# Trailing-window sums of the pooling branch on VectorE instead of GpSimd, issued 28 passes behind their product

## The chip, the cores and the metric

The kernel runs on one NeuronCore of a Trainium2 chip. The core has a matrix engine (TensorE, PE in the profile), a vector engine (VectorE, DVE), an activation engine (ScalarE, ACT), a general-purpose engine (GpSimd, POOL) and a queue engine that issues the loads (SyncE, SP). Each of them works through its own instructions strictly in order, and they wait for one another through semaphores. The metric is the device time of one execution in microseconds (us), as the median of several runs.

## The reference

Two layers of a streaming encoder over 512 tokens of 1024 channels in float32. Each layer is a feed-forward block, a mixer and another feed-forward block. The mixer adds up three branches, each behind a gate; the change lies in branch B, the pooling one:

```
def multiscale_pool(u, w_pool, pool_scale):        # u = h @ w_in[:, columns of B], 512 columns
    for g, w in enumerate((2, 4, 8, 16)):          # four groups of 128 channels
        # mean of the last w tokens (fewer at the start), minus the token itself
        diffs.append((upper - lower) / count - uf[:, :, sl])
    y = jnp.einsum('bsgc,gce->bsge', d, w_pool)    # one 128 x 128 map for each group
    return y * pool_scale
...
branch = jnp.einsum('bsnw,nwd->bsnd', ys, w_branch)
gates = jax.nn.sigmoid(g_lin.reshape(B, S, N_BRANCHES, D_MODEL))
merged = jnp.sum(gates * branch, axis=2)
return merged @ w_out
```

## The kernel before

Channels lie on the 128 partitions and tokens on the free axis, so a tile is 128 x 512. To keep float32 accuracy on TensorE, every operand is split in two parts, a rounded one (`whi`, `hhi`) and the rest (`wlo`, `hlo`), and each product takes three matmuls (`triple`, L119 to L121). A 128-column product over 1024 channels is eight triples, or 24 matmuls; the code counts a matmul of 512 columns as one pass in `pe[0]`.

`wchunk` brings one block of weights: a load into `raw` (two buffers), a ScalarE cast to `whi` (L277) and a VectorE subtraction to `wlo` (L279). `whi` and `wlo` have three buffers each. The sums of the products stand in PSUM tiles called `acc`, of which there are four.

`later(n, fn)` puts a piece of work on a list, and `poll`, called before every triple, runs whatever is due once `n` passes have been recorded. Behind this recording stands a scheduler that sets the final order of each engine's instructions by priorities; so the order on an engine is not the order of the code.

At the end of each mixer stand, in this order: the four pooling groups (`pool_front`), the merge of branch C (`merge_units(l, 2, ...)`: for each of eight column blocks a gate product of 24 passes and a branch product of 12) and the merge of branch B. A pooling group is a product into an `acc` tile; a ScalarE copy of it to `u` (L1027), with 16 zero columns ahead; log2(w) additions of `u` with itself shifted by 1, 2, 4, 8 columns (L1033, tiles `strip`, two buffers), that is 1, 2, 3 and 4 additions for the groups 0 to 3; the division and the difference (L1037 to L1040); a split into `ptb` (L384, L385). Sixty passes later `pool_back` multiplies it by its map (three matmuls into another `acc` tile), and ScalarE and VectorE empty that tile (L1050, L1051).

In the same stretch the kernel works ahead on the modulation of later blocks: `mod_step` loads 512 KB of `w_ada` into a tile `b` and reduces it on VectorE (L206). These loads stand in the same SP queue as the weight loads.

The chosen lines of the change:

```
        nc.scalar.copy(u[:, 16:], pu)
...
            nc.gpsimd.tensor_tensor(nx[:, 16:], cur[:, 16:], cur[:, 16 - step:T + 16 - step], op=ALU.add)
...
            for gi in range(4):
                b = pool_front(l, gi)
                later(60, lambda gi=gi, b=b: pool_back(l, gi, b, wp, yb))
```

Of the kernel before, what the change touches and what calls it, by code (L numbers as in the profile page):

```python
# [19 lines left out]
ALU = mybir.AluOpType  # L20
# [3 lines left out]
T = 512  # L24
# [11 lines left out]
WINDOWS = (2, 4, 8, 16)  # L36
# [4 lines left out]
def encoder_kernel(tc, xT, c, w_ada, b_ada, gains, w_gate, w_up, w_down, w_qkv, w_f, w_ubg,  # L41
                   qk_gain, rel, fbias, w_pool, pool_scale, w_branch, w_out, inv_cnt, w_first, out):
    nc = tc.nc
# [54 lines left out]
    def later(delay, fn, group=None):  # L98
        t = Task(pe[0] + delay, fn, group)
        tasks.append(t)  # L100
        return t
# [160 lines left out]
    def wchunk(src, shape, side=True, spare=None, lo_eng=None):  # L262
        lo_eng = lo_eng or nc.vector
        side_work(side)
        raw = st([P] + list(shape), F32, *(("b", NB) if spare else ("raw", NRAW)))
        last["dma"] = nc.sync.dma_start(raw, src).ins
        if spare == "ptb":
            both = st([P, 2] + list(shape), F32R, "ptb", 2)
            hi, lo = both[:, 0], both[:, 1]
        elif spare == "b":  # L270
            hi = st([P] + list(shape), F32R, "b", NB)
            lo = st([P] + list(shape), F32R, "b", NB)
        else:
            hi = st([P] + list(shape), F32R, "whi", 3)
            lo = st([P] + list(shape), F32R, "wlo", 3)
        with behind("scalar"):
            nc.scalar.copy(hi, raw)  # L277
        with behind("vector"):
            lo_eng.tensor_tensor(lo, raw, hi.bitcast(F32), op=ALU.subtract)  # L279
        return hi, lo  # L280
# [735 lines left out]
    LAG_T, LAG_V = 30, 14  # L1016


    def pool_front(l, g):
        w = WINDOWS[g]  # L1020
        hi, lo = wchunk(w_ubg[l, g], (KD, P))
        pu = acc()
        for k in range(KD):
            triple(pu, hi[:, k, :], lo[:, k, :], hhi[:, k, :], hlo[:, k, :], k == 0, k == KD - 1)
        u = st([P, T + 16], F32, "b", NB)
        nc.gpsimd.memset(u[:, :16], 0.0)
        nc.scalar.copy(u[:, 16:], pu)  # L1027
        cur = u
        step = 1
        while step < w:  # L1030
            nx = st([P, T + 16], F32, "strip", 2)
            nc.gpsimd.memset(nx[:, :16], 0.0)
            nc.gpsimd.tensor_tensor(nx[:, 16:], cur[:, 16:], cur[:, 16 - step:T + 16 - step], op=ALU.add)  # L1033
            cur = nx
            step *= 2
        hd = st([P, 16], F32, "hd", 1)
        nc.vector.tensor_tensor(hd, cur[:, 16:32], icnt[:, g, :], op=ALU.mult)  # L1037
        df = st([P, T], F32, "ssum", 1)
        nc.vector.scalar_tensor_tensor(df[:, 16:], cur[:, 32:], 1.0 / w, u[:, 32:], op0=ALU.mult, op1=ALU.subtract)
        nc.vector.tensor_tensor(df[:, :16], hd, u[:, 16:32], op=ALU.subtract)  # L1040
        b = st([P, 2, T], F32R, "ptb", 2)
        split_to(b[:, 0, :], b[:, 1, :], df)
        return b

    def pool_back(l, g, b, wp, ys):
        py = acc()
        triple(py, wp[0][:, g, :], wp[1][:, g, :], b[:, 0, :], b[:, 1, :], True, True)
        y = blk("b")
        sc = psc[:, l, g:g + 1]
        nc.scalar.activation(y[:, 0, :], py, AF.Identity, scale=sc)  # L1050
        nc.vector.scalar_tensor_tensor(y[:, 1, :], py, sc, y[:, 0, :].bitcast(F32), op0=ALU.mult, op1=ALU.subtract)  # L1051
        ys.append(y)
# [9 lines left out]
    def merge_units(l, n, ys, put):  # L1062
        wb = [None]
        gates = {}

        def gate_of(d):
            if d % 2 == 0:
                wb[0] = wchunk(w_branch[l, n, d:d + 2].rearrange("a p k c -> p a k c"), (2, 4, P))
            gh, gl = wchunk(w_ubg[l, 4 + n * KD + d], (KD, P))
            pg = gates[d] = acc()  # L1070
            for k in range(KD):
                triple(pg, gh[:, k, :], gl[:, k, :], hhi[:, k, :], hlo[:, k, :], k == 0, k == KD - 1)
                yield

        for d in range(KD):
            if d not in gates:
                yield from gate_of(d)
            if n == 0 and d == 0:
                yield from gate_of(1)
            pg = gates[d]  # L1080
            bh, bl = wb[0]
            th = t1(T)
            nc.scalar.activation(th, pg, AF.Tanh, scale=0.5)
            pb = acc()
            if n == 0 and d == 0:
                poll(group="a")
            for k in range(4):
                triple(pb, bh[:, d % 2, k, :], bl[:, d % 2, k, :], ys[k][:, 0, :], ys[k][:, 1, :], k == 0, k == 3)
                yield
            put(d, pb, th)  # L1090
# [6 lines left out]
    class Mixer:  # L1097
# [10 lines left out]
        def run(self, nxt):  # L1108
            l = self.l
            in_ffn[0] = False  # L1110
            for b in range(4):
                nc.gpsimd.dma_start(x_dram[b], x_blocks[b].rearrange("p a t -> p (a t)"))
            g = qkgc[:, l, :]
            g8 = qg8[:, l, :]
            qa, ka, va, qc, kc, vc = [], [], [], [], [], []
            ya, yb, yc = [], [], []
            drain(proj_qk(l, 0, g8[:, 0:1], True, qa, self.pre, self.norm),
                  proj_qk(l, 1, g[:, 1:2], False, ka), forget(l),
                  proj_v(l, 2, "xv", va))
            finish_turns()  # L1120
            turns.clear()
            heads[0] = 0

            def fill_a():
                yield from proj_qk(l, 3, g8[:, 2:3], True, qc)
                yield from proj_qk(l, 4, g[:, 3:4], False, kc)
                yield from proj_v(l, 5, "v2", vc)

            attention(qa, ka, va, lambda h: strip_a(l, h), ya, fill_a(), FILL_A, "a")
            heads[0] = H  # L1130

            m = []

            def put_a(d, pb, th):
                if d % 2 == 0:
                    m.append(blk("xv", F32))
                nc.vector.scalar_tensor_tensor(m[d // 2][:, d % 2, :], th, 1.0, pb, op0=ALU.add, op1=ALU.mult)

            def put_c(d, pb, th):
                md = m[d // 2][:, d % 2, :]  # L1140
                tmp = t2(T)
                nc.vector.scalar_tensor_tensor(tmp, th, 1.0, pb, op0=ALU.add, op1=ALU.mult)
                nc.gpsimd.tensor_tensor(md, md, tmp, op=ALU.add)

            mh = []

            def put_b(d, pb, th):
                put_c(d, pb, th)
                b = blk("v2" if d < 4 else "b")
                split_to(b[:, 0, :], b[:, 1, :], m[d // 2][:, d % 2, :])  # L1150
                mh.append(b)

            ubs = {}

            def fill_c():
                yield from merge_units(l, 0, ya, put_a)

            attention(qc, kc, vc, lambda h: strip_c(l, h), yc, fill_c(), FILL_C, "c")
            finish_turns()
            turns.clear()  # L1160
            poll(True)
            silc[0] = st([P, D], F32, "b", NB)
            nc.sync.dma_start(silc[0], sil_dram.broadcast_to([P, D]))
            wp = wpool_load(l)
            mc = merge_units(l, 2, yc, put_c)
            for gi in range(4):
                b = pool_front(l, gi)
                later(60, lambda gi=gi, b=b: pool_back(l, gi, b, wp, yb))
            in_ffn[0], mod_tag[0], MOD_RATE[0] = True, "b", 1.0
            drain(mc)  # L1170
            poll(True)
            mb = merge_units(l, 1, yb, put_b)
            drain(mb)
            in_ffn[0], mod_tag[0] = False, "raw"

            for b in range(4):
                xb = blk("xv", F32)
                nc.sync.dma_start(xb, x_dram[b].rearrange("p (a t) -> p a t", a=2))
                x_blocks[b] = xb
            mod_need(l, 5)  # L1180
            for c0 in (0, T):
                def src(c):
                    return w_out[l, 2 * c * P:(2 * c + 2) * P, c0:c0 + T].rearrange("(k p) c -> p k c", p=P)

                def ops(hi, lo, kt, j):
                    return (hi[:, j * P:(j + 1) * P], lo[:, j * P:(j + 1) * P], mh[kt][:, 0, :], mh[kt][:, 1, :])

                if c0 == 0:
                    nxt.prefetch("b")
                for j, hs, o in k_outer(src, 4, ops, nxt.prefetch_weights if c0 else None):  # L1190
                    d = c0 // P + j
                    residual_tail(d, hs, o, modc[:, l, 5, d:d + 1], nxt)
# [69 lines left out]
```

## Time and profile before

| what | value |
|---|---|
| time, median of 3 runs | 2403.73 us (2403.13 to 2406.02) |
| time of the profiled execution | 2404.73 us |
| its span | 2403.0 us |
| granted TensorE clock | 1.00 |
| busy: PE, DVE, ACT, POOL | 2359.9, 1725.9, 1198.4, 351.7 us |
| the pooling additions (L1033), both layers | 20 on POOL, 1.04 to 1.90 us each |
| loads over the span | 320.94 MB, mean 134 GB/s |

Busy time is the union of the instructions' spans on an engine. A row of the timeline gives start, length, engine, line, operation, tiles (written <- read) and shape; in square brackets at its end stands how long the engine sat idle before it and who ended that. Matmuls overlap in the pipeline: one of 512 columns is shown as 0.39 us long, but in a stretch without waits the next one starts 0.23 us after it. A time lost on PE is therefore read from the distance of two starts.

### The profile page before, as it was taken

Reading aid. Unit: us, or ns where it says so; the run is one execution under the profiler, and the core shown is the slowest. Engines: PE = TensorE matmul, PEld = TensorE weight load, DVE = VectorE, ACT = ScalarE, POOL = GpSimd, SP = SyncE. Lnnn points to the kernel's source line nnn. Section 1 sums busy time; section 2 is a strip of 40 time slices with the busy share of each in tenths; the row PEclk is TensorE's granted clock in tenths of the full one; section 3 lists DMA queues with packets and bytes.
Section 4 is the critical chain, followed back from the end, with each engine's and each line's share of the span. In section 5 each row is a group of like instructions: output and inputs, shape, how many; then the busy total and the mean of one; then the engine's idle time right before and its main releaser. Section 6 shows DMA issues by size and latency. Waiting matters only on the chain. (4 is left out here: it accounts for less than half of the span.)

```text
span 2403.0 us, 36815 instructions
## 1 busy us (share of the span) xinstructions
PE 2359.9 (98%) x14106; PEld 2085.6 (87%) x14106; DVE 1725.9 (72%) x3070; ACT 1198.4 (50%) x2090; POOL 351.7 (15%) x423
## 2 busy tenths in 40 slices
PE   7999999999999999999999999999999999999999
PEld 5799998778878898989998989978787788989898
DVE  8988866787665476878677878577866655658583
ACT  5353555786632353535553626466865324536252
POOL 3000011144432210000100000102444322000000
PEclk9999999999999999999999999999999999999999
DMA  7736342323345424353325353423233554223322
GB/s 274 238 113 228 99 152 84 93 79 109 108 171 201 175 98 166 105 186 105 132 83 196 104 197 106 141 79 98 80 116 108 193 182 169 71 97 106 101 96 103
DMA packets 116438, 320.94 MB, mean 134 GB/s; under 512 B 11139, under 2 KB 13315, under 8 KB 116261
## 3 DMA queue, kind: packets, MB, share of 16 engines
q1 hardware_dynamic: 115106, 314.38, 38.7%
q0 software_dynamic: 1152, 4.19, 0.4%
q8 instruction: 111, 1.82, 0.3%
q14 instruction: 67, 0.54, 0.1%
q10 hardware_dynamic: 2, 0.00, 0.0%
HBM read 312.16 MB, written 6.38 MB: 133 GB/s over the span
## 5 line engine op out<-in xcount | busy, mean ns | idle before, releaser
L277 ACT CAST whi<-raw 128x1024 fp32r<-128x1024 f32 (+1 forms) x267 | 277.4, 1043 | 431.5 <-PE acc L120 217.9
L279 DVE TENSOR_TENSOR wlo<-raw,whi 128x1024 fp32r<-128x1024 f32 x259 | 319.4, 1237 | 162.2 <-ACT whi L277 159.0
L119 PE MATMUL acc<-b,whi 128*128 128x512 f32 (+1 forms) x960 | 360.7, 376 | 0.2 <-DVE xv L434 0.2
L121 PE MATMUL acc<-b,wlo 128*128 128x512 f32 (+1 forms) x960 | 356.7, 372 | 1.8 <-DVE wlo L279 1.8
L120 PE MATMUL acc<-b,whi 128*128 128x512 f32 (+1 forms) x960 | 357.1, 372 | 0.0
L121 PEld LDWEIGHTS acc<-b,wlo 128*128 128x128 f32 x960 | 180.8, 188 | 34.0 <-DVE wlo L279 2.6
L119 PEld LDWEIGHTS acc<-b,whi 128*128 128x128 f32 x960 | 180.8, 188 | 31.8 <-DVE xv L434 0.6
L120 PEld LDWEIGHTS acc<-b,whi 128*128 128x128 f32 x960 | 181.0, 189 | 29.8
L119 PE MATMUL acc<-hhi,whi 128*128 128x512 f32 x480 | 191.3, 400 | 6.8 <-DVE b L1051 3.1
L121 PE MATMUL acc<-hhi,wlo 128*128 128x512 f32 x480 | 188.1, 393 | 1.0 <-DVE wlo L279 1.0
L120 PE MATMUL acc<-hlo,whi 128*128 128x512 f32 x480 | 188.6, 393 | 0.2 <-DVE hlo L711 0.2
L384 ACT CAST ptb<-v 128x1024 fp32r<-128x1024 f32 x128 | 134.0, 1050 | 97.7 <-DVE v L452 56.2
L385 DVE TENSOR_TENSOR ptb<-v,ptb 128x1024 fp32r<-128x1024 f32 x128 | 156.3, 1223 | 33.8 <-ACT ptb L384 32.3
L384 ACT CAST whi<-raw 128x1024 fp32r<-128x1024 f32 (+1 forms) x128 | 106.7, 834 | 92.1 <-PE acc L120 41.9
L119 PE MATMUL acc<-whi,hhi 128*128 128x512 f32 x336 | 137.8, 411 | 0.9 <-DVE xv L385 0.9
L206 DVE CUSTOM_DVE_ANT_0 v<-v,b,badac 128x1024 f32<-128x1024 f32 x96 | 127.1, 1333 | 15.0 <-DMA v<-in_w_ada_dram 14.8
L121 PE MATMUL acc<-whi,hlo 128*128 128x512 f32 x336 | 131.9, 393 | 0.0
L120 PE MATMUL acc<-wlo,hhi 128*128 128x512 f32 x336 | 131.6, 392 | 0.0
L385 DVE TENSOR_TENSOR wlo<-raw,whi 128x1024 fp32r<-128x1024 f32 (+1 forms) x128 | 121.6, 950 | 6.5 <-ACT whi L384 5.0
L434 DVE SCALAR_TENSOR_TENSOR xv<-acc,modc,xv 128x512 f32<-128x512 f32 (+1 forms) x112 | 77.3, 690 | 62.2 <-PE acc L121 62.0
L119 PEld LDWEIGHTS acc<-hhi,whi 128*128 128x128 f32 x480 | 90.6, 189 | 25.6 <-DVE b L1051 4.0
L329 POOL TENSOR_TENSOR ssum<-ssum,t 128x256 f32<-128x256 f32 (+1 forms) x45 | 46.5, 1034 | 442.8 <-ACT t L328 442.7
(315 smaller groups left out, 6667.5 us busy)
## 6 DMA issues: line engine op xcount, KB each, us to landing
v<-in_w_ada_dram SPq DMA_DIRECT2D x96, 512.0 KB, 5.3
raw<-in_w_down_dram SPq DMA_DIRECT2D x88, 512.0 KB, 3.7
raw<-in_w_up_dram SPq DMA_DIRECT2D x82, 512.0 KB, 4.0
raw<-in_w_gate_dram SPq DMA_DIRECT2D x79, 512.0 KB, 3.7
raw<-in_w_ubg_dram SPq DMA_DIRECT2D x56, 512.0 KB, 3.6
b<-in_w_ada_dram SPq DMA_DIRECT2D x48, 512.0 KB, 4.6
raw<-in_w_qkv_dram SPq DMA_DIRECT2D x42, 512.0 KB, 3.9
raw<-in_w_branch_dram SPq DMA_DIRECT2D x24, 512.0 KB, 3.7
```

The source lines that it names most:

```text
L119: mm(o, lh, rh, start=start, stop=False)
L120: mm(o, lh, rl, start=False, stop=False)
L121: mm(o, ll, rh, start=False, stop=stop)
L206: dot = nc.vector.tensor_tensor_reduce(out=raw, in0=raw, in1=silc[0], scale=1.0, scalar=badac[:, l, j, d:d + 1], op0=ALU.mult, op1=ALU.add ...
L277: nc.scalar.copy(hi, raw)
L279: lo_eng.tensor_tensor(lo, raw, hi.bitcast(F32), op=ALU.subtract)
L329: nc.gpsimd.tensor_tensor(self.ssum[:, cols], self.ssum[:, cols], q, op=ALU.add)
L384: nc.scalar.copy(hi, src)
L385: nc.vector.tensor_tensor(lo, src, hi.bitcast(F32), op=ALU.subtract)
L434: nc.vector.scalar_tensor_tensor(x, acc_j, gate, x, op0=ALU.mult, op1=ALU.add)
```

## The change

`pool_front` is cut in two. `pool_in` holds the product, the zero columns and the ScalarE copy to `u`; it is recorded for the four groups directly one after the other. The rest (`pool_front` with `u`, run by `pooled`) is recorded 28 passes after the end of the group's product, and `pool_back` 30 passes after that instead of 60 after the product. The additions go to VectorE; the small memsets of the zero columns stay on GpSimd.

```diff
-    def pool_front(l, g):
-        w = WINDOWS[g]
+    def pool_in(l, g):
         hi, lo = wchunk(w_ubg[l, g], (KD, P))
         pu = acc()
...
         nc.scalar.copy(u[:, 16:], pu)
+        return u
+
+    def pool_front(l, g, u):
+        w = WINDOWS[g]
         cur = u
...
-            nc.gpsimd.tensor_tensor(nx[:, 16:], cur[:, 16:], cur[:, 16 - step:T + 16 - step], op=ALU.add)
+            nc.vector.tensor_tensor(nx[:, 16:], cur[:, 16:], cur[:, 16 - step:T + 16 - step], op=ALU.add)
...
+            us = []
+
+            def pooled(gi):
+                b = pool_front(l, gi, us[gi])
+                later(30, lambda: pool_back(l, gi, b, wp, yb))
+
             for gi in range(4):
-                b = pool_front(l, gi)
-                later(60, lambda gi=gi, b=b: pool_back(l, gi, b, wp, yb))
+                us.append(pool_in(l, gi))
+                later(28, lambda gi=gi: pooled(gi))
```

From the copy to `u` on, line numbers of the changed kernel differ: the copy is L1026, the addition L1036, the difference L1040 to L1043, the emptying of `pool_back`'s tile L1053 (ScalarE) and L1054 (VectorE), the emptying of a gated branch product L1145.

What the scheduler makes of it is seen engine by engine. On PE all matmuls stand in the same sequence as before: four products of 24 with `pool_back` of group 0 in the middle of the fourth, then the first gate product with that of group 1 in it, the first branch product with that of group 2, the second gate product with that of group 3. VectorE's queue is what moves.

VectorE before, layer 0, from the split of group 2 to the emptying of group 1's tile. `wlo_1510` is the weight of the second gate product, `strip_1487` the last sum of group 3, `acc_1500` the tile of group 1's map, and `b_1491` and `b_1495` are `w_ada` loads:

```order
L385 TENSOR_TENSOR ptb_1476_7250<-ssum_1475_7247,ptb_1476_7250 128x512
L279 TENSOR_TENSOR wlo_1510_7395<-raw_1508_7392,whi_1509_7394 128x1024
L206 ISA b_1491_7314,modc_123<-b_1491_7314,b_1444_7102,badac_104 128x1024
L206 ISA modc_123 128x1
L206 ISA b_1495_7323,modc_123<-b_1495_7323,b_1444_7102,badac_104 128x1024
L206 ISA modc_123 128x1
L1037 TENSOR_TENSOR hd_1488_7306<-strip_1487_7303,icnt_111 128x16
L1039 SCALAR_TENSOR_TENSOR ssum_1489_7308<-strip_1487_7303,b_1483_7291 128x496
L1040 TENSOR_TENSOR ssum_1489_7308<-hd_1488_7306,b_1483_7291 128x16
L1051 SCALAR_TENSOR_TENSOR b_1501_7346<-acc_1500_7342,psc_109,b_1501_7346 128x512
L385 TENSOR_TENSOR ptb_1490_7311<-ssum_1489_7308,ptb_1490_7311 128x512
L279 TENSOR_TENSOR wlo_1520_7454<-raw_1518_7451,whi_1519_7453 128x1024
```

VectorE now, the same place. The sums of group 3 are `strip_1497` to `strip_1500`, the tile of group 1's map is `acc_1493`, and the `w_ada` loads are `b_1478` and `b_1482`:

```order
L385 TENSOR_TENSOR ptb_1492_7313<-ssum_1491_7310,ptb_1492_7313 128x512
L1036 TENSOR_TENSOR strip_1497_7350<-b_1477_7274 128x512
L206 ISA b_1478_7277,modc_123<-b_1478_7277,b_1444_7102,badac_104 128x1024
L206 ISA modc_123 128x1
L206 ISA b_1482_7286,modc_123<-b_1482_7286,b_1444_7102,badac_104 128x1024
L206 ISA modc_123 128x1
L1054 SCALAR_TENSOR_TENSOR b_1494_7326<-acc_1493_7322,psc_109,b_1494_7326 128x512
L1036 TENSOR_TENSOR strip_1498_7353<-strip_1497_7350 128x512
L279 TENSOR_TENSOR wlo_1510_7395<-raw_1508_7392,whi_1509_7394 128x1024
L1036 TENSOR_TENSOR strip_1499_7356<-strip_1498_7353 128x512
L1036 TENSOR_TENSOR strip_1500_7359<-strip_1499_7356 128x512
L279 TENSOR_TENSOR wlo_1520_7454<-raw_1518_7451,whi_1519_7453 128x1024
```

The emptying of group 1's tile has moved ahead of group 3's difference, and the weight `wlo_1510` has moved behind the two `w_ada` reductions, this emptying and two sums.

VectorE before, directly behind that, to the weight `wlo_1524` of the third gate product (`acc_1504` and `acc_1512` are the tiles of the maps of groups 2 and 3, `acc_1503` that of the first branch product):

```order
L1051 SCALAR_TENSOR_TENSOR b_1505_7377<-acc_1504_7373,psc_109,b_1505_7377 128x512
L1142 SCALAR_TENSOR_TENSOR t2_1506_7386<-t1_1502_7364,acc_1503_7366 128x512
L206 ISA b_1507_7389,modc_123<-b_1507_7389,b_1444_7102,badac_104 128x1024
L206 ISA modc_123 128x1
L1051 SCALAR_TENSOR_TENSOR b_1513_7421<-acc_1512_7417,psc_109,b_1513_7421 128x512
L279 TENSOR_TENSOR wlo_1524_7463<-raw_1522_7460,whi_1523_7462 128x1024
```

VectorE now, the same place (`acc_1496` is the first branch product):

```order
L1040 TENSOR_TENSOR hd_1501_7362<-strip_1500_7359,icnt_111 128x16
L1042 SCALAR_TENSOR_TENSOR ssum_1502_7364<-strip_1500_7359,b_1477_7274 128x496
L1043 TENSOR_TENSOR ssum_1502_7364<-hd_1501_7362,b_1477_7274 128x16
L1054 SCALAR_TENSOR_TENSOR b_1505_7377<-acc_1504_7373,psc_109,b_1505_7377 128x512
L1145 SCALAR_TENSOR_TENSOR t2_1506_7386<-t1_1495_7344,acc_1496_7346 128x512
L385 TENSOR_TENSOR ptb_1503_7367<-ssum_1502_7364,ptb_1503_7367 128x512
L206 ISA b_1507_7389,modc_123<-b_1507_7389,b_1444_7102,badac_104 128x1024
L206 ISA modc_123 128x1
L1054 SCALAR_TENSOR_TENSOR b_1513_7421<-acc_1512_7417,psc_109,b_1513_7421 128x512
L279 TENSOR_TENSOR wlo_1524_7463<-raw_1522_7460,whi_1523_7462 128x1024
```

Group 3's difference and split now stand behind `wlo_1520` instead of ahead of it; from the `w_ada` reduction of `b_1507` on, VectorE's order is the old one again. Layer 1 is changed in the same way.

## The prediction

> **What bounds the kernel now.** I read the page first, for what could be won at all:
>
> ```profile
> span 2403.0 us, 36815 instructions
> PE 2359.9 (98%) x14106; PEld 2085.6 (87%) x14106; DVE 1725.9 (72%) x3070; ACT 1198.4 (50%) x2090; POOL 351.7 (15%) x423
> ```
>
> TensorE is without work for 43.1 of 2403.0 us, over the whole kernel. The change leaves all its matmuls and their sequence as they are, so it can win only what PE waits for in the pooling stages. The waits of PE, longest in total first, give one line for them:
>
> ```profile
> PE acc L119 <- DVE b L1051: 3.1, 2, 1.6
> ```
>
> Two waits, 3.1 us in all, at the emptying of a map's tile by VectorE. The timeline of PE shows both, at the start of the second gate product of branch C in each layer:
>
> ```profile
> 692.13 0.40 PE L120 MATMUL acc<-b,whi 128*128 128x512 f32 x1
> 692.36 0.40 PE L121 MATMUL acc<-b,wlo 128*128 128x512 f32 x1
> 694.33 0.50 PE L119 MATMUL acc<-hhi,whi 128*128 128x512 f32 x1 [1.57 <-DVE b L1051]
> 694.66 0.40 PE L120 MATMUL acc<-hlo,whi 128*128 128x512 f32 x1
> ...
> 1878.29 0.40 PE L121 MATMUL acc<-b,wlo 128*128 128x512 f32 x1
> 1880.26 0.50 PE L119 MATMUL acc<-hhi,whi 128*128 128x512 f32 x1 [1.57 <-DVE b L1051]
> ```
>
> Starts are 0.23 us apart where nothing waits (692.13 to 692.36). Here they are 1.97 apart, and the first matmul after the pause takes 0.33. So each wait costs 1.97 - 0.23 + 0.33 - 0.23 = 1.84 us. Why is VectorE late? Its timeline, then GpSimd's, from the same stretch:
>
> ```profile
> 686.37 2.06 DVE L206 CUSTOM_DVE_ANT_0 b<-b,b,badac 128x1024 f32<-128x1024 f32 x1
> ...
> 692.76 0.17 DVE L1037 TENSOR_TENSOR hd<-strip,icnt 128x16 f32<-128x16 f32 x1 [2.34 <-POOL strip L1033]
> 692.86 0.67 DVE L1039 SCALAR_TENSOR_TENSOR ssum<-strip,b 128x496 f32<-128x496 f32 x1
> ...
> 693.53 0.75 DVE L1051 SCALAR_TENSOR_TENSOR b<-acc,psc,b 128x512 fp32r<-128x512 f32 x1
> ```
>
> ```profile
> 685.82 1.53 POOL L1033 TENSOR_TENSOR strip<-b 128x512 f32<-128x512 f32 x1 [2.20 <-ACT b L1027]
> 687.43 1.90 POOL L1033 TENSOR_TENSOR strip<-strip 128x512 f32<-128x512 f32 x1
> ...
> 689.46 1.86 POOL L1033 TENSOR_TENSOR strip<-strip 128x512 f32<-128x512 f32 x1
> ...
> 691.44 1.29 POOL L1033 TENSOR_TENSOR strip<-strip 128x512 f32<-128x512 f32 x1
> ```
>
> The four sums of group 3 occupy GpSimd from 685.82 to 692.73. VectorE's next instruction, L1037, waits for them 2.34 us, and behind it stands the emptying L1051, which runs only from 693.53 to 694.28. It frees the PSUM tile in which the gate product begins at 694.33.
>
> **The change, part by part.** *Removed from GpSimd:* 20 sums. Nothing else stands in GpSimd's queue there but the small memsets of the zero columns.
>
> *Added to VectorE:* ten sums in each layer. No row shows one there. The nearest rows are the VectorE groups between 655 and 716 us, the same shape from two SBUF tiles (L385) and the same shifted operands at 496 columns (L1039); the other rows are wanted below. The upper bound is a split that ran while GpSimd was adding:
>
> ```profile
> L1051 DVE SCALAR_TENSOR_TENSOR b<-acc,psc,b 128x512 fp32r<-128x512 f32 x4 | 3.0, 749 | 1.2 <-ACT b L1050 1.2
> L385 DVE TENSOR_TENSOR ptb<-ssum,ptb 128x512 fp32r<-128x512 f32 x4 | 2.8, 692 | 1.5 <-ACT ptb L384 1.4
> L1039 DVE SCALAR_TENSOR_TENSOR ssum<-strip,b 128x496 f32<-128x496 f32 x4 | 2.7, 666 | 0.0
> L1142 DVE SCALAR_TENSOR_TENSOR t<-t,acc 128x512 f32<-128x512 f32 x3 | 2.0, 679 | 0.0
> L1040 DVE TENSOR_TENSOR ssum<-hd,b 128x16 f32<-128x16 f32 x4 | 0.7, 167 | 0.0
> ```
>
> ```profile
> 668.12 1.53 DVE L385 TENSOR_TENSOR pta<-t,pta 128x512 fp32r<-128x512 f32 x1
> ```
>
> A sum is 0.69 to 1.53 us; I take 0.69, because GpSimd has only memsets left in the stretch. The Trainium skill (Perfetto Trace Analysis, Optimizing Scalar/DVE Operations) warns that moving work between these two engines might not help, since they share an SBUF read port. This trace agrees on the sharing (1.53 against 0.69 for a split), but by that sentence the gain would be about nothing, where the rows below give 3.7 us, because the bound engine is neither of the two.
>
> Does VectorE have the room? The busy time of each engine (PE, PEld, DVE, ACT, POOL) from 655 to 695 us:
>
> ```profile
> 655.00:695.00 40.00, 37.10 (x172) 30.09 (x171) 24.32 (x40) 16.23 (x28) 17.44 (x22) 1.00 0.37 125
> ```
>
> 24.3 of 40 us, plus 10 x 0.69 = 6.9, is 31.2. There is room; what matters is the order.
>
> *Moved on VectorE:* the emptying of group 1's tile goes ahead of group 3's difference, and the second gate's weight goes behind two w_ada reductions. The rows for that chain in layer 0 are three weight splits of VectorE (the first gate's, the second gate's, the next branch's) and a reduction that doesn't run beside GpSimd, then ScalarE's cast and copy:
>
> ```profile
> 678.24 1.23 DVE L279 TENSOR_TENSOR wlo<-raw,whi 128x1024 fp32r<-128x1024 f32 x1 [0.26 <-ACT whi L277]
> ...
> 685.23 1.23 DVE L279 TENSOR_TENSOR wlo<-raw,whi 128x1024 fp32r<-128x1024 f32 x1 [0.26 <-ACT whi L277]
> ...
> 695.30 1.23 DVE L279 TENSOR_TENSOR wlo<-raw,whi 128x1024 fp32r<-128x1024 f32 x1 [0.26 <-ACT whi L277]
> ...
> 702.85 1.28 DVE L206 CUSTOM_DVE_ANT_0 b<-b,b,badac 128x1024 f32<-128x1024 f32 x1
> ...
> 704.05 0.08 DVE L206 DVE_READ_ACCUMULATOR2_ANT modc<- 128x1 f32 x1
> ```
>
> ```profile
> 683.62 0.62 ACT L384 CAST ptb<-ssum 128x512 fp32r<-128x512 f32 x1 [2.50 <-DVE ssum L1040]
> ...
> 685.10 0.58 ACT L1027 COPY b<-acc 128x512 f32<-128x512 f32 x1
> ```
>
> I lay them end to end, which is a little too long (L1039 above starts 0.10 after a 0.17 us L1037). The first gate's split ends at 679.47. Three sums of group 2, 2.07: 681.54. Its L1037-like step 0.17, the emptying of group 0's tile 0.75, difference 0.67 + 0.17: 683.30. Cast 0.62 and split 0.69: 684.61; ScalarE's copy of group 3 meanwhile ends at 684.50. First sum of group 3, 0.69: 685.30. Two w_ada reductions, 2 x (1.28 + 0.08 for the accumulator): 688.02. Emptying of group 1's tile: 688.77. Without the wait the gate product starts at 692.36 + 0.23 = 692.59, so the tile is free 3.8 us early and **the wait goes**.
>
> What is late next? Sum 0.69 and gate weight 1.23: 690.69, needed by the third matmul at 693.05, 2.4 early. Two sums 1.38, next weight 1.23, group 3's 0.17 + 0.67 + 0.17: 694.31. Two emptyings 0.75 + 0.68 beside the cast: 695.74. Split 0.69: 696.43. It is needed by group 3's map:
>
> ```profile
> 698.76 0.40 PE L120 MATMUL acc<-ptb,pta 128*128 128x512 f32 x1
> ```
>
> That is 4.43 after the gate's start at 694.33, 0.10 of which is the slow first matmul, so it comes at 692.59 + 4.33 = 696.92: 0.49 us early. This is the tightest place.
>
> *The w_ada loads* stand ahead of all that. SP's timeline (two issues in one row) and the page's median from issue to landing:
>
> ```profile
> 679.97 0.89 SPq L203 DMA_DIRECT2D b<-in_w_ada_dram  x2
> ```
>
> ```profile
> b<-in_w_ada_dram SPq DMA_DIRECT2D x48, 512.0 KB, 4.6
> ```
>
> They are issued behind the split that ends at 679.47 in both kernels, and land at about 685, when VectorE comes for them. The only bound that the timeline shows is 686.37, where VectorE takes the first without a wait. From there all of the above is 1.07 later: tile and gate weight still in time, the map 0.58 late. So each layer gains 1.26 to 1.84 us; I take 1.84, since the end-to-end sum already errs by about that.
>
> *Moved on SP:* the load of the third gate's weight waits until the second gate's weight is split, to 690.7 instead of 686.5; its cast has to wait for the end of the second gate product, 27 matmuls or 6.2 us after 692.59, so that hides it. The loads behind it wait for the next branch's weight, to 693.3 instead of 696.5, and go earlier. ScalarE's copies to u no longer stand behind a cast that waits for GpSimd. Group 0 and 1's sums fill VectorE's old waits. These I cost at nothing.
>
> *Sum:* 2 x 1.84 = 3.7 us. The profiled execution took 2404.73 us, its span plus 1.7 around it, 1.0 above the median of 2403.73. So 2401.0 for such an execution, and a median of **2400.1**.
>
> **The rivals.** *A second wait goes with it.* In layer 1, 27 us later, PE waits for a weight behind a late w_ada load:
>
> ```profile
> 1905.81 0.39 PE L120 MATMUL acc<-hlo,whi 128*128 128x512 f32 x1
> 1907.15 0.50 PE L121 MATMUL acc<-hhi,wlo 128*128 128x512 f32 x1 [0.95 <-DVE wlo L279]
> ```
>
> ```profile
> 1898.20 6.45 DMA b<-in_w_ada_dram
> ```
>
> Starts 1.34 apart cost 1.11, plus 0.11 for the slow matmul: 1.2 us. The load took 6.45 us against a median of 4.6, and layer 0 shows no such wait. If the four loads that now go earlier thin the traffic, it goes: 2398.9. Against it: the load itself is issued as before relative to PE.
>
> *The tile stays the limit.* All four acc tiles are held at that moment in both kernels (first gate, map 1, first branch, map 2). If another release comes last, the wait keeps its place: up to 2403.7. For it: the same 1.57 in both layers. The Trainium skill (Perfetto Trace Analysis, Optimization Strategy) reads a repeating gap on the saturated engine as possibly too little PSUM, and no tile is added. By that rule nothing is won. Against it: 3.8 us to spare.
>
> *Slower: VectorE becomes what PE waits for at group 3's map.* If the sums ran at the 1.53 us of the slowed split, the seven sums of groups 2 and 3 would cost 7 x 0.84 = 5.9 more, 5.4 past the 0.49 to spare; 2 x 5.4 - 3.7 = 7.1 us slower, 2410.8. It turns into a loss from (1.84 + 0.49) / 7 = 0.33 more, 1.02 us for each sum. For it: nothing but that row. Against: the row lies beside a GpSimd sum, and there are none left. A w_ada landing after 687.2 would make PE wait there too.
>
> **How the numbers follow.** Forecast 0.55, second wait gone too 0.26, tile the limit 0.10, VectorE late 0.09. Two thousandths, 4.8 us, is about what a measurement of this kernel can tell from no change, so a gain of 3.7 lies within it. Faster by more: half of the second case and a little of the first, 0.20. Slower by more: 0.09. Within: 0.71. The range reaches from 2398.0, the second case and a little less, to 2403.4, most of the third.
>
> **What would show it.** Right: no wait of PE on L1054; sums of about 0.69 us on VectorE; the next matmul at group 3's map without a gap; PE's idle time down by 3 us. Wrong: a wait of PE on the split of group 3 (L385) or on the second gate's weight, or sums of over 1 us.

## The result, and the profile after

The changed kernel takes 2399.14 us (median of 14 runs, 2396.56 to 2402.36) against 2403.62 for the kernel before, run beside it (14 runs, 2401.51 to 2406.57): a ratio of 0.9983, 95% interval 0.9976 to 0.9989, or 2.6 to 5.8 us. The profiled execution took 2397.95 us, with a span of 2396.2. A few single executions came out far slower (one of E7's eleven and two of E10's seven below, and two of the kernel before, at 3314 to 8879 us), and all medians and ratios are of the others.

The head of its page answers to the first lines shown of before:

```profile
span 2396.2 us, 36811 instructions
PE 2358.4 (98%) x14106; PEld 2086.2 (87%) x14106; DVE 1736.1 (72%) x3090; ACT 1199.5 (50%) x2090; POOL 325.2 (14%) x403
```

PE is without work for 37.8 us instead of 43.1. Its timeline at the two places that the prediction named, with group 3's map of layer 0 between them:

```profile
691.62 0.39 PE L121 MATMUL acc<-b,wlo 128*128 128x512 f32 x1
691.85 0.39 PE L119 MATMUL acc<-hhi,whi 128*128 128x512 f32 x1
...
695.93 0.40 PE L119 MATMUL acc<-ptb,pta 128*128 128x512 f32 x1
696.16 0.40 PE L120 MATMUL acc<-ptb,pta 128*128 128x512 f32 x1
...
1874.16 0.39 PE L121 MATMUL acc<-b,wlo 128*128 128x512 f32 x1
1874.39 0.39 PE L119 MATMUL acc<-hhi,whi 128*128 128x512 f32 x1
```

The second gate products (691.85, 1874.39) start 0.23 behind the matmul in front of them, where it was 1.97. VectorE in layer 0 shows why:

```profile
683.56 0.69 DVE L1036 TENSOR_TENSOR strip<-b 128x512 f32<-128x512 f32 x1
684.16 1.28 DVE L206 CUSTOM_DVE_ANT_0 b<-b,b,badac 128x1024 f32<-128x1024 f32 x1
...
686.58 0.75 DVE L1054 SCALAR_TENSOR_TENSOR b<-acc,psc,b 128x512 fp32r<-128x512 f32 x1
687.24 0.68 DVE L1036 TENSOR_TENSOR strip<-strip 128x512 f32<-128x512 f32 x1
687.84 1.22 DVE L279 TENSOR_TENSOR wlo<-raw,whi 128x1024 fp32r<-128x1024 f32 x1
...
693.52 0.68 DVE L385 TENSOR_TENSOR ptb<-ssum,ptb 128x512 fp32r<-128x512 f32 x1
```

The emptying of group 1's tile (L1054) ends at 687.33, 4.5 us ahead of the gate product that takes the tile; before, it ended at 694.28 and the product waited for it. Group 3's split ends at 694.20, and the map's second matmul, which reads it, comes at 696.16. The groups of lines from 653 to 715 us give what a sum costs on VectorE, and what is left of the wait ahead of L1037, now L1040:

```profile
L1036 DVE TENSOR_TENSOR strip<-strip 128x512 f32<-128x512 f32 x6 | 4.1, 688 | 0.3
...
L1036 DVE TENSOR_TENSOR strip<-b 128x512 f32<-128x512 f32 x4 | 2.7, 685 | 0.0
...
L1040 DVE TENSOR_TENSOR hd<-strip,icnt 128x16 f32<-128x16 f32 x4 | 0.7, 174 | 0.1
```

Because PE's matmuls stand in the same sequence in all these kernels, two traces can be compared matmul by matmul: a jump in the difference of their start times is time won or lost at that place. From before to after the jumps at the two places are -1.85 each (-1.73 at the first matmul behind the pause and the rest at the next one, which had been 0.33 behind it instead of 0.23), so **3.7 us** were won there. The spans differ by 6.8; the other 3.1 lie at places that the change does not touch, and one more, below.

### The profile page after: what moved, and what is told of

The parts are those of the page before. It is cut to its first block, busy times and chain, and to the rows that moved or that the text cites. A ratio compares the mean times of both kernels' runs of the same rounds, so it can differ in the third digit from the quotient of the medians.

```text
span 2396.2 us, 36811 instructions
## 1 busy us (share of the span) xinstructions
PE 2358.4 (98%) x14106; PEld 2086.2 (87%) x14106; DVE 1736.1 (72%) x3090; ACT 1199.5 (50%) x2090; POOL 325.2 (14%) x403
## 5 line engine op out<-in xcount | busy, mean ns | idle before, releaser
L119 PE MATMUL mm<-hhi,whi 128*128 128x512 f32 x280 | 109.5, 392 | 1.4 <-ACT whi L277 1.4
```

Of the source, the lines that this page charges most:

```text
L119: mm(o, lh, rh, start=start, stop=False)
```

## The experiments

| run | what runs | median us | ratio to before, 95% interval | jumps at the two second gate products |
|---|---|---|---|---|
| E1 | sums on VectorE, no delay | 2400.20 | 0.9985 (0.9975 to 0.9994) | -1.85, -1.85 |
| E13 | the same again | 2398.45 | 0.9980 (0.9971 to 0.9989) | -1.85, -1.85 |
| E2 | the delay, sums on GpSimd | 2400.54 | 0.9985 (0.9976 to 0.9994) | -1.85, -1.85 |
| E3 | group 3's sums alone on VectorE | 2400.10 | 0.9982 (0.9973 to 0.9991) | -1.85, -1.85 |
| E4 | before, maps in the other PSUM pool | 2399.80 | 0.9989 (0.9980 to 0.9998) | -1.85, -1.85 |
| E5 | before, one sum for group 3 | 2399.48 | 0.9980 (0.9971 to 0.9989) | -1.85, -1.85 |
| E7 | changed, maps in the other PSUM pool | 2400.32 | 0.9979 (0.9970 to 0.9988) | -1.85, -1.85 |
| E8 | changed, GpSimd adding beside | 2406.38 | 1.0012 (1.0003 to 1.0021) | -1.85, -1.85, then losses |
| E9 | changed, memsets on VectorE | 2398.02 | 0.9976 (0.9967 to 0.9984) | -1.85, -1.85 |
| E10 | E9, GpSimd adding beside | 2412.79 | 1.0039 (1.0025 to 1.0054) | both waits gone, then losses |

The ratios are to runs of before on the same chip beside each group, and the jumps are to the first trace of before. E11 and E12 are second traces of before and after. No run bears the number E6.

**E1, the engine without the delay.**

```diff
-            nc.gpsimd.tensor_tensor(nx[:, 16:], cur[:, 16:], cur[:, 16 - step:T + 16 - step], op=ALU.add)
+            nc.vector.tensor_tensor(nx[:, 16:], cur[:, 16:], cur[:, 16 - step:T + 16 - step], op=ALU.add)
```

> The kernel before with one word changed: the pooling sums on VectorE, issued where they were, without the delay of 28 passes. Theory (the wait at the second gate product is the emptying of group 1's tile, which stands on VectorE behind group 3's difference, which waits for GpSimd): the fast sums alone let VectorE reach the emptying in time, so both waits of 1.57 us go, PE's steps at the two places fall from 1.97 to about 0.23 us, and the time falls by 3.5 us, as with the full change. Rival (the delay is what does it): the waits stay, time within 1 us of before. Rival (VectorE becomes late): sums of over 1 us, PE waits on the split of group 3, time above before.

Both waits went. VectorE's timeline shows the emptying of group 1's tile at 689.75, between two sums of group 3, and PE took the tile at 692.94:

```profile
689.75 0.74 DVE L1051 SCALAR_TENSOR_TENSOR b<-acc,psc,b 128x512 fp32r<-128x512 f32 x1
690.41 0.68 DVE L1033 TENSOR_TENSOR strip<-strip 128x512 f32<-128x512 f32 x1
```

So the delay is not needed for this gain. But the scheduler has moved the emptying here too, ahead of group 3's last sum and difference. Whether faster sums would do with the emptying left behind that difference, no run shows.

**E2, the delay without the engine.** The changed kernel with `nc.gpsimd.tensor_tensor` in that line.

> The changed kernel with its sums back on GpSimd: the delay alone. In VectorE's order the emptying of group 1's tile now stands ahead of group 3's difference. Theory (it is the place in VectorE's order, not GpSimd's speed, that makes the wait): the emptying runs before the gate product needs the tile (by about 691.2 against 692.6 in layer 0), the two waits of 1.57 us go, about 3.5 us faster than before although GpSimd still adds for 1.0 to 1.9 us at a time; reductions of VectorE beside these sums stay at about 2.06 us. Rival (GpSimd's speed itself bounds PE here): PE waits as long somewhere else in the stretch, at group 3's map, time as before.

Both waits went as well. VectorE, then GpSimd, then PE in layer 0:

```profile
691.05 0.74 DVE L1054 SCALAR_TENSOR_TENSOR b<-acc,psc,b 128x512 fp32r<-128x512 f32 x1
693.46 0.17 DVE L1040 TENSOR_TENSOR hd<-strip,icnt 128x16 f32<-128x16 f32 x1 [1.67 <-POOL strip L1036]
```

```profile
690.16 1.86 POOL L1036 TENSOR_TENSOR strip<-strip 128x512 f32<-128x512 f32 x1
...
692.14 1.28 POOL L1036 TENSOR_TENSOR strip<-strip 128x512 f32<-128x512 f32 x1
```

```profile
693.07 0.39 PE L121 MATMUL acc<-b,wlo 128*128 128x512 f32 x1
693.30 0.39 PE L119 MATMUL acc<-hhi,whi 128*128 128x512 f32 x1
```

GpSimd is as slow as before (1.86 and 1.28 us), VectorE's reductions still take 2.06 us beside it, and VectorE still waits 1.67 us for it, but the emptying now stands ahead of that wait and ends at 691.79, and PE goes on at 693.30 without a gap. The place in VectorE's queue is enough, without any gain in the speed of either engine.

**E3, eight sums of twenty.** `(nc.vector if g == 3 else nc.gpsimd).tensor_tensor(...)` in the kernel before.

> The kernel before with only group 3's four additions of each layer on VectorE; groups 0 to 2 stay on GpSimd. Theory: only group 3's sums stand ahead of the emptying that PE waits for, so eight moved instructions of twenty bring the whole gain: both waits of 1.57 us gone, 3.5 us faster than before. Rival (GpSimd's load as a whole slows VectorE, or the gain is spread over the stretch): a part of it only, under 2 us.

Jumps of -1.85 and -1.85, the whole 3.7 us, and a median like the others'. The other twelve moved sums bring nothing at these places. As in E1, the emptying stands ahead of group 3's last sum and difference here.

**E4, another tile for the maps.**

```diff
-        py = acc()
+        py = mmt()
```

> The kernel before, where the maps' results go to a tile of the other PSUM pool instead of one of the four acc tiles; the sums stay on GpSimd and the order on VectorE as it was. Rival of the prediction (the four acc tiles are the limit): the gate product finds another tile free and the two waits of 1.57 us go, 3.5 us faster, although VectorE empties group 1's tile as late as before (693.5 to 694.3 in layer 0). Theory (VectorE blocked behind GpSimd): this takes away the reason why PE needs the emptying, so it says the same for the wait at this place, and tells only that nothing else of PE's needs VectorE there; if VectorE's late group 3 work is itself needed, PE waits for its split of group 3 instead and less than 1 us is won.

VectorE and PE in layer 0:

```profile
693.40 0.17 DVE L1037 TENSOR_TENSOR hd<-strip,icnt 128x16 f32<-128x16 f32 x1 [2.33 <-POOL strip L1033]
...
694.16 0.74 DVE L1051 SCALAR_TENSOR_TENSOR b<-mm,psc,b 128x512 fp32r<-128x512 f32 x1
```

```profile
693.01 0.39 PE L121 MATMUL acc<-b,wlo 128*128 128x512 f32 x1
693.24 0.39 PE L119 MATMUL acc<-hhi,whi 128*128 128x512 f32 x1
```

VectorE waits 2.33 us for GpSimd and empties the tile as late as before (694.16), and PE starts at 693.24 all the same. So the tile is a link of the chain: PE needed that emptying only because it needed the tile. Nothing else of VectorE's late work stopped PE there. Further on in layer 0 of this trace, 26 us behind the gate product, PE did wait 0.67 us for a weight, which no other trace shows in that layer (more on such waits below).

**E5, a shorter chain on GpSimd.** `while step < (2 if g == 3 else w)` in the kernel before.

> The kernel before with one addition on GpSimd for group 3 in place of four (this leaves out three of its four window sums, so group 3's means cover two tokens instead of sixteen); nothing is put on VectorE. Theory (VectorE's wait for group 3's chain on GpSimd is the cause): the chain ends about 5 us earlier, VectorE doesn't wait at group 3's difference, both PE waits of 1.57 us go, 3.5 us faster than before. Rival (the acc tiles or the w_ada loads set the place): the waits stay.

-1.85 and -1.85: with nothing added to VectorE the waits go. VectorE still waits 0.93 us for GpSimd at group 3's difference, where no wait was expected. The scheduler has put that difference ahead of the two reductions, and the emptying behind it ends at 693.59, 0.70 ahead of the gate product. E1, E2, E4 and E5 cut the same chain at different links (the slow sums, the order behind them, the tile, the number of sums), and each brings the whole of it. In E1 and E5 the scheduler changed the order as well, so E2 and E4 are the ones that cut a single link.

**E7, the changed kernel with the other tile too.** The edit of E4 on the changed kernel.

> The changed kernel, and the maps' results in the other PSUM pool as well. Theory (after the change the tile is free 4.5 us before it is needed): nothing left to win, within 1 us of the changed kernel. Rival (the tile shortage still costs something in the stretch): faster than the changed kernel by 1 us or more.

2400.32 us, 0.9979: not to be told from the changed kernel. Behind the change no cost of the tiles is left that this comparison can show.

**E8, a neighbour for the sums.** In the changed kernel the zero columns of `strip` are set by VectorE, and ahead of each sum stands:

```diff
+            for c in range(16, T + 16, P):
+                nc.gpsimd.tensor_tensor(scr, u[:, c:c + P], u[:, c - step:c - step + P], op=ALU.add)
```

> The changed kernel with GpSimd kept adding columns of u beside VectorE's sums (its results are used by nobody; the zero columns are set by VectorE), four additions of 128 columns for each sum. Rival of the prediction (sums beside GpSimd's traffic run at up to 1.53 us and VectorE gets late at group 3's map): sums at 1.5 us, w_ada reductions at 2.06; seven sums of groups 2 and 3 cost 5.9 us more, of which the 1.96 us to spare that the changed kernel's trace shows before group 3's map hides that much, so 3.9 us of PE waits in each layer, 7.9 us slower than the changed kernel. Theory (the neighbour is what would have slowed them, but it was gone): the same direction, sums between 0.69 and 1.53 us; PE waits only if they pass 0.69 + 1.96 / 7 = 0.97 us. If the sums stay at 0.69 us, the slowed split of before had another cause.

7.2 us over the changed kernel, close to the rival's 7.9, but not on its way. The sums ran at 0.69 to 0.89 us, not at 1.5. VectorE and PE in layer 0:

```profile
687.42 0.69 DVE L1039 TENSOR_TENSOR strip<-b 128x512 f32<-128x512 f32 x1 [1.77 <-POOL b L1026]
688.03 1.42 DVE L207 CUSTOM_DVE_ANT_0 b<-b,b,badac 128x1024 f32<-128x1024 f32 x1
```

```profile
698.72 0.51 PE L119 MATMUL acc<-ptb,pta 128*128 128x512 f32 x1 [1.32 <-ACT ptb L385]
699.54 0.50 PE L120 MATMUL acc<-ptb,pta 128*128 128x512 f32 x1 [0.32 <-DVE ptb L386]
```

PE did wait at group 3's map, but part of the cause was made by the experiment: VectorE waited 1.77 us for a memset of group 3's `u` (L1026) that stood in GpSimd's queue behind the added work. The time matched and the mechanism did not, so it was tried again without that memset.

**E9, its control.** Both memsets (`u` and `nx`) of the changed kernel are `nc.vector.memset`.

> Control for the next run: the changed kernel with the small memsets of the zero columns on VectorE, nothing added on GpSimd. Both theories: 14 memsets of about 0.07 us in each layer, of which 7 stand between the sums of groups 2 and 3, 0.5 us against the 1.96 us that the changed kernel's trace shows to spare before group 3's map: no wait of PE there, within 1 us of the changed kernel, sums at 0.69 us, w_ada reductions at 1.28.

2398.02 us, no wait at group 3's map. Its interval overlaps that of the changed kernel, so no gain of its own is shown.

**E10, the neighbour alone.** VectorE's order is the control's; ahead of each sum stands, with a bfloat16 `scr`:

```diff
+            for c in (16, 16 + 2 * P):
+                nc.gpsimd.tensor_tensor(scr, u[:, c:c + 2 * P], u[:, c - step:c - step + 2 * P], op=ALU.add)
```

> The control with GpSimd adding columns of u beside each sum of VectorE (two additions of 128 x 256, results used by nobody), and VectorE waiting for nothing of GpSimd's: it takes away the 1.77 us for which VectorE waited for GpSimd's memset in e8, and leaves the neighbour. VectorE's order is the control's. From the end of the w_ada loads to group 3's split VectorE has about 10 us of work. If it is slowed as in e8 (weight split 1.42 against 1.23, factor 1.15), that is 1.6 us more, within what is to spare: no or little wait of PE at group 3's map, within 1 us of the control; then e8's loss came from the memset. If it is slowed as in the kernel before (reduction 2.06 against 1.28, factor 1.6), it is 6 us more, 4 us of PE waits in each layer at group 3's map, 8 us slower than the control.

14.8 us slower than the control, nearly twice the larger of the two expected sizes. VectorE in layer 0, a 16-column step, a reduction, an emptying and a weight split beside GpSimd's additions:

```profile
676.94 0.58 DVE L1046 TENSOR_TENSOR ssum<-hd,b 128x16 f32<-128x16 f32 x1
...
688.19 1.64 DVE L207 CUSTOM_DVE_ANT_0 b<-b,b,badac 128x1024 f32<-128x1024 f32 x1
...
691.32 0.74 DVE L1057 SCALAR_TENSOR_TENSOR b<-acc,psc,b 128x512 fp32r<-128x512 f32 x1
691.98 1.12 DVE L1039 TENSOR_TENSOR strip<-strip 128x512 f32<-128x512 f32 x1
693.02 1.63 DVE L280 TENSOR_TENSOR wlo<-raw,whi 128x1024 fp32r<-128x1024 f32 x1
```

```profile
694.70 0.50 PE L121 MATMUL acc<-hhi,wlo 128*128 128x512 f32 x1 [1.59 <-DVE wlo L280]
...
700.19 0.50 PE L119 MATMUL acc<-ptb,pta 128*128 128x512 f32 x1 [1.57 <-ACT ptb L385]
702.02 0.50 PE L120 MATMUL acc<-ptb,pta 128*128 128x512 f32 x1 [1.34 <-DVE ptb L386]
```

The rival's mechanism exists: PE waits for the second gate's weight and for group 3's split. The size can be followed. Measured from the gate product, VectorE began group 3's sums 3.2 us later than in the control (687.13 against 692.49, there 683.55 against 692.08). From there to the end of the split it took 14.84 us instead of 10.95, 3.9 more. Less the control's 1.9 us to spare at the map, that is 5.2; the jumps on PE from the control to E10 are +1.87, +1.73 and +1.70, 5.3. Not all of it is the added work's: 1.1 of the 3.9 is group 3's split, which ran beside an addition that GpSimd makes in the changed kernel too, that of the first gated branch product to `xv`:

```profile
700.17 1.80 DVE L386 TENSOR_TENSOR ptb<-ssum,ptb 128x512 fp32r<-128x512 f32 x1
```

```profile
700.16 1.26 POOL L1149 TENSOR_TENSOR xv<-xv,t 128x512 f32<-128x512 f32 x1 [3.79 <-DVE t L1148]
```

Then comes a price that nobody had set. The windows of E10 behind these waits (busy time of PE, PEld, DVE, ACT, POOL, the granted clock, DMA):

```profile
698.00:702.00 4.00, 1.12 (x4) 0.37 (x2) 3.91 (x8) 0.62 (x1) 1.26 (x1) 1.00 0.99 363
...
703.20:706.70 3.50, 3.50 (x11) 2.68 (x10) 1.99 (x3) 1.83 (x3) 0.00 (x0) 0.52 0.77 305
```

Behind 4 us in which PE was busy for 1.12, its granted clock was 0.52 over 3.5 us, and matmuls started 0.43 apart, not 0.23, which cost another 1.6. Each layer lost about 7.0, both 13.9 of the 16.3 us between the two profiled spans (2410.9 and 2394.6).

**E11 and E12, second traces of before and of after.**

> The kernel before, unchanged, for a second trace. Theory (the two waits at the second gate product belong to the order of instructions): both again, steps of 1.97 us. The wait for a weight in layer 1, 27 us later (1.2 us), and two waits of the last feed-forward block of layer 0 (0.6 us each), were chance if they come with another size or not at all; if they come as before, they belong to the kernel before.

> The changed kernel, unchanged, for a second trace. Theory: steps of 0.23 us at both second gate products again, group 3's split about 2 us early. Whether the layer 1 wait for a weight, which the first trace of the changed kernel didn't have, stays away: if it does here and comes in the second trace of the kernel before, the change takes it away as a second gain; if it comes back, it was chance.

PE in layer 1, second trace of before, then of after:

```profile
1878.66 0.50 PE L119 MATMUL acc<-hhi,whi 128*128 128x512 f32 x1 [1.55 <-DVE b L1051]
...
1905.31 0.50 PE L121 MATMUL acc<-hhi,wlo 128*128 128x512 f32 x1 [0.67 <-DVE wlo L279]
```

```profile
1873.24 0.39 PE L121 MATMUL acc<-b,wlo 128*128 128x512 f32 x1
1873.47 0.39 PE L119 MATMUL acc<-hhi,whi 128*128 128x512 f32 x1
```

The two waits at the second gate products belong to the kernel before; the jumps in the second trace of after are -1.85 and -1.85, 3.7 together again. The wait for a weight 27 us later came in both traces of before and in neither of after. The two waits in the feed-forward block (-0.67 and -0.69 from before to before again) are chance: unchanged code lost them, and the two spans of the same kernel differ by 3.1 us.

**E13, E1 once more**, for that wait for a weight.

> The sums on VectorE without the delay, a second time, for the layer 1 wait for a weight, which was there in this kernel's first trace (0.83 us) and in both of the kernel before (0.95 and 0.67), and not in six of kernels with the delay. If the delay is what takes it away, it comes again here, at 0.6 to 1 us, and the time is 2400, 1 us above the changed kernel; if it is gone here, it is chance, and nothing separates this kernel from the changed one.

This time the wait was not there, in the kernel that had shown 0.83 us of it. Its two traces settle that it can come and go with no change of code.

## Why the prediction was right, step by step

- **Forecast and result.** 2400.1 was said and 2399.14 came, inside the range of 2398.0 to 2403.4, and within 0.2% of before as the 0.71 had it. The 3.7 us of its sum came at the two places that it named; what the medians show beyond that (4.5, with 2.6 to 5.8 as the interval) is not told apart from chance.
- **The two waits, 1.84 us each.** Measured 1.85 at each place, in both traces of after. The cause that was named (an emptying in order behind a wait for GpSimd) is shown by E2, which changes when the work is issued and leaves the engines as they were, its link through the tile by E4, and E1, E3 and E5 agree with it.
- **A sum at 0.69 us.** 0.68 to 0.69 for all twenty. The bound of 1.53 was for a neighbour that had left, and none came beside the sums. But it was not so that GpSimd had only memsets left in the stretch: its addition of the first gated branch product to `xv` started 0.16 us behind group 3's split (693.52), which kept its 0.68 us, while the next reduction was slowed to 2.32:

```profile
693.68 1.67 POOL L1146 TENSOR_TENSOR xv<-xv,t 128x512 f32<-128x512 f32 x1 [3.85 <-DVE t L1145]
```

```profile
694.12 2.32 DVE L206 CUSTOM_DVE_ANT_0 b<-b,b,badac 128x1024 f32<-128x1024 f32 x1
```

  The working had not foreseen this addition, so that the split began first was luck, though of little price: at E10's 1.80 us it would have eaten 1.1 of the 1.96 us to spare.
- **The spare time: mis-sized.** The working gave 3.8 us at the tile, 2.4 at the gate's weight and 0.49 at group 3's map, the "tightest place". Measured: 4.5, 3.2 and 1.96. Laying rows end to end was the fault: the rows of after start 0.60 behind a 0.69 us sum (683.56 to 684.16), and nearly every instruction of the chain overlaps the next by about 0.1 us. Over some fifteen of them that is the 1.5 us.
- **The second wait goes too (0.26).** This is what both traces of after show, and 2398.9 is nearer to the result than the forecast. Its reason, that loads issued earlier would thin the traffic, fell: in E1 the four `w_ada` loads were issued at 1877.63, 0.3 us ahead of the gate product, and the wait was there; in E4 they came at 1881.82, 4.3 behind it, and only 0.06 us of it was left. What does go with it is how long the last load ahead of that weight takes. The chains of waits of E11 (a wait of 0.67 us), E3 (0.41) and E4 (0.06) name it:

```profile
1896.63 6.17 DMA b<-in_w_ada_dram
```

```profile
1895.17 5.90 DMA b<-in_w_ada_dram
```

```profile
1895.64 5.23 DMA b<-in_w_ada_dram
```

  No kernel with the delay showed the wait (seven traces), and five of seven traces without it did, with E4's 0.06 us. The counts lean towards the delay making it rarer, but E5 and E13 were free of it without the delay and no mechanism was found, so this stays open.
- **The tile stays the limit (0.10).** Half of it was true: E4 wins the same by a tile alone. But a late emptying and a scarce tile are one chain, and cutting it anywhere is enough; E7 finds nothing left. The rule weighed there (the Trainium skill, Perfetto Trace Analysis, Optimization Strategy: a repeating gap may be too little PSUM) names a true link, and E4's jumps of -1.85 and -1.85 are what it is worth; it does not follow that nothing is won without a tile.
- **VectorE late at group 3's map (0.09).** The place and the wait were right, as E10 shows, the price was not: it counted 0.84 us on seven sums. In E10 all but the last of the sums took 0.94 to 1.19 us, weight splits and reductions were slowed too, GpSimd's own addition hit the split, and behind the waits PE's clock was low.
- **The shared port.** The other rule weighed (the Trainium skill, Perfetto Trace Analysis, Optimizing Scalar/DVE Operations: moving work between these engines might not help) did not decide here, since the gain came out of an order and not out of either engine's busy time; E2 wins it with both as slow as before.

## What to carry to other kernels

Read a wait back through the in-order queue of the engine that releases it: what stood in front of the releasing instruction, and whom did that wait for? Such a chain can be cut at any link, and the cheapest cut (a tile, one place in the order) may do the work of a move between engines. Before a difference of a few us is explained from two traces, take a second trace of the unchanged kernel: here it moved by 3.1 us by itself.

## What the hardware showed that was not expected

- **Where a neighbour slows an instruction, it adds about a fixed time, not a factor.** Beside GpSimd's additions of 256 columns (E10) VectorE's 16-column step took 0.58 us instead of 0.17, its sums of `u` 1.10 instead of 0.69, its weight split 1.63 instead of 1.22, its reduction 1.64 instead of 1.28: about 0.4 more, whatever the length. Beside 128 columns (E8) it was up to about 0.2 (1.42 for the split), and beside the 512-column sums of the kernel before 0.8 (reduction 2.06, split 1.53); beside the 512-column addition to `xv` it was 1.0 to 1.1 (reduction 2.32, E10's split 1.80). The emptying, with one operand in PSUM, stayed at 0.74. The Trainium skill (SBUF — State Buffer, Who interferes with whom) fits the emptying: an instruction with two SBUF inputs contends with a GpSimd instruction that reads SBUF, one with a single SBUF input does not. Several rows don't follow from that alone: the 496-column difference (L1045) reads two SBUF tiles and kept its 0.66 us in all twelve cases in E8 and E10 in which GpSimd was adding, and in E8 two of group 3's sums kept 0.69. Why was not tried.
- **Idle time on PE can cost more than it lasts.** Waits of 1.57 us alone left the clock as it was in the kernel before, whose window behind the first of them shows it full:

```profile
694.00:698.00 4.00, 3.67 (x16) 3.08 (x17) 3.66 (x6) 2.34 (x4) 0.14 (x1) 1.00 0.08 17
```

  In E8 waits of 1.32 and 0.32 within 1 us were followed by a clock of 0.50 for 3.4 us in layer 0 (699.9 to 703.3), and in layer 1, with the same waits, the clock stayed at 1.00. The Trainium skill (TensorE: Matmul & The Clock Gate, What's actually happening) ascribes such a drop to an idle window of about 3.4 us that runs freely; the length of the slow stretch agrees (3.4 us in E8 and in both layers of E10), but at none of these places was PE idle for that long in one piece.
